# An encoder layer on eight cores: a wider last row block, late queueing of gated products on VectorE, and one more wait on GpSimd

## The chip, the cores and the metric

One Trainium2 chip (trn2), all 8 cores, one launch. The time is the device time of the slowest core in microseconds. A core's span runs from its first to its last instruction in a profiled execution. Some executions fall in a slow state, in which one die runs at a lower clock; only fast runs are compared here, and every profile shown is of a fast run.

## The reference

One layer over x of 4 x 4096 x 1024, float32:

```python
x = x + 0.5 * swiglu(rmsnorm(x, ffn1_norm), ffn1_gate, ffn1_up, ffn1_down)   # hidden 2816
z = rmsnorm(x, mix_norm) @ w_in                                             # q, k, v (512 each), u (1024)
attn_out = chunk_band_attention(q, k, v, rel_bias)                          # 64-row chunks, 576 keys
conv_out = conformer_conv(u, dw_kernel, dw_bias, conv_ln_g, conv_ln_b)      # GLU, conv of 31, LayerNorm, swish
x = x + concatenate([attn_out, conv_out]) @ w_out
x = x + 0.5 * swiglu(rmsnorm(x, ffn2_norm), ffn2_gate, ffn2_up, ffn2_down)
y = rmsnorm(x, final_norm)
```

## The kernel before

Two cores share a sequence. An even core does its first 2176 rows, an odd core the other 1920 and a halo of 512. Rows go through the layer in two groups, and a group in blocks of up to 512 rows, the columns of a matmul:

```python
PLANS = ((((512, False), (384, False), (256, False)),      # even core: group 0
          ((512, False), (256, False), (256, False))),     #            group 1
         (((512, True), (512, False), (256, False)),       # odd core, True is the halo
          ((512, False), (384, False), (256, False))))
```

A Python scheduler holds one stream of work for each part of the layer, estimates the time of each engine, and writes five static instruction queues with semaphore waits. Queues are in order: what stands first in a queue holds up all behind it (the prediction shows a stop of 3.65 us on VectorE that came of it). Where it expects TensorE to wait, it puts filler matmuls.

An FFN piece and a GLU piece each end in an activation on ScalarE and a product on VectorE, which the kernel before queues at once:

```python
ti = nxt("tmpF", 2)
tt = tmpF[:, ti, 0:n]
act(tt, gb, AF.Silu, n, (("ps", bG),), (("tmpF", ti),))
dve(lambda h: h.tensor_tensor(out=at, in0=ub, in1=tt, op=ALU.mult), n,
    (("ps", bU), ("tmpF", ti)), (("AT", gi, fl, s),))
# ... in glu(): channel pieces c, row runs r
todo = [(c, r) for part in (early, late) for c in (0, 1) for r in part]
todo += [(c, r) for c in (2, 3) for r in runs]
# ...
act(tt, bb, AF.Tanh, n, (("ps", bB),), (("rs", ti),), scale=0.5)
dve(lambda h: h.scalar_tensor_tensor(out=gnt, in0=tt, scalar=1.0, in1=ab_,
    op0=ALU.add, op1=ALU.mult), n, (("ps", bA), ("rs", ti)), (("gn", gi_),))
```

After its GLU a group sends the result through DRAM to change its layout, and the convolution reads it back; the scheduler assumes that the return lands 4 us after its bytes. During the first FFN, GpSimd expands the convolution weights, 8 instructions of 4 us, while VectorE writes tables for the attention bias:

```python
P.op("pool", lambda h: h.tensor_tensor(out=o_, in0=i0, in1=i1, op=ALU.mult), 4.1,
     ("cmp", "i32"), (("cwb", i % 2),))                    # waits for i32 only
# ... setup_tables()
dve(lambda h: h.tensor_scalar(out=dst, in0=src, scalar1=rbc, scalar2=None, op0=ALU.subtract), 192,
    ("stage", "cs"), ("cb",))
```

The softmax here doesn't subtract the row's maximum and nothing guards it: scores larger than these inputs give would overflow.

## Time and profile before

| | before |
|---|---|
| time, median of 6 (of all 15 with later rounds; of the 12 fast ones of these) | 1378.92 us (1378.2; 1377.9) |
| spans of the even cores 0, 2, 4, 6 | 1374.7, 1375.3, 1376.2, 1376.4 us |
| spans of the odd cores 1, 3, 5, 7 | 1364.2, 1365.9, 1363.5, 1364.5 us |
| TensorE busy, core 6 | 97% |

The prediction shows most of the lines that matter. Two more kinds are needed later. The first is the view by windows: the stretch, its length, the busy time of TensorE (with instructions), of weight loads, VectorE, ScalarE and GpSimd, then the granted TensorE clock. This is core 6 just after its 3.4 us stop:

```profile
83.80:86.00 2.20, 2.18 (x7) 1.01 (x8) 0.34 (x1) 0.46 (x1) 0.00 (x0) 0.50 1.05 322
```

The clock, third number from the end, is 0.50: after the stop TensorE works at half speed ("half clock" below). The second is an odd core, core 1, where its first convolution begins; the timeline has start, length, instruction, and in brackets the engine's idle time before it and what ended that:

```profile
366.83 5.37 PE L502 MATMUL ps<-dreg,ring 128*128 128x192 bf16 x43 [2.26 <-DMA dreg<-gscr]
```

TensorE waits 2.3 us for the layout's return. In the window 364.0 to 370.4 us of this core the clock was 0.82: the first 16 matmuls came 0.083 us apart, the next 20 came 0.16 us apart, and then they were 0.083 us apart again. So half clock can set in after the stop is over.

### The profile page before, as it was taken

What the parts mean: (1) busy time and instruction counts of PE and PEld (TensorE: products, weight loads), DVE (VectorE), ACT (ScalarE), POOL (GpSimd) and SP (SyncE); (2) the same over time, 40 slices, a digit from 0 to 9 for tenths busy, and PEclk for the clock granted to TensorE, in tenths of its full rate; (3) what the DMA queues carried; (4) which work ended last, traced back from release to release, by engine and by line L of the source; (5) the groups of instructions that cost most, each with busy time, mean ns of one, the idle gap of its engine ahead of it and who ended that gap; (6) DMA issues with size and microseconds to landing.
All of it is one profiled execution on the core that took longest, in us unless ns stands there. A gap on an engine that the chain in (4) does not pass through costs nothing.

```text
span 1376.4 us, 25529 instructions; the slowest of 8 cores (1363.5 to 1376.4 us)
## 1 busy us (share of the span) xinstructions
PE 1337.3 (97%) x9485; PEld 843.3 (61%) x9485; DVE 490.0 (36%) x904; ACT 445.4 (32%) x843; POOL 252.3 (18%) x303
## 2 busy tenths in 40 slices
PE   8999999999999999999999999999999999999995
PEld 4556655565655665656656766766675567666654
DVE  4442222362644432222254522225345253222225
ACT  4311011252477631001245410124438763100123
POOL 2064000340402320000062000006040220000022
PEclk9999999999999999999999999999999999999998
DMA  9386326254740182343311864453674006335413
GB/s 224 72 172 150 62 35 123 43 111 121 160 101 1 33 214 53 71 92 70 70 32 32 213 140 86 75 92 64 151 154 101 18 2 123 64 68 92 81 20 125
DMA packets 33632, 127.72 MB, mean 93 GB/s; under 512 B 3424, under 2 KB 11744, under 8 KB 26464
## 3 DMA queue, kind: packets, MB, share of 16 engines
q0 software_dynamic: 18752, 96.10, 37.0%
q1 hardware_dynamic: 14752, 29.92, 6.8%
q8 instruction: 80, 1.31, 0.4%
q14 instruction: 48, 0.39, 0.1%
HBM read 191.95 MB, written 18.09 MB: 153 GB/s over the span
## 4 chain that ended last, share of the span: by engine, by line
PE 88%; DMA 4%; DVE 3%; issue 2%; ACT 1%; POOL 1%; SPq 0%; DVEq 0%; ACTq 0%; POOLq 0%
PE psA L502 52%; PE ps L502 37%; DMA ring<-wgu 2%; DMA dreg<-gscr 1%; DVE hT L752 1%; DMA gscr<-dreg 1%; DVE xres L752 1%; ACT dreg L512 0%; DVE xres L1415 0%; ACT pb L512 0%; ACT L510 0%; SPq L976 0%; DVE xres L925 0%; DMA xres<-xin 0%; POOL xres L639 0%
## 5 line engine op out<-in xcount | busy, mean ns | idle before, releaser
L502 PE MATMUL psA<-hT,ring 128*128 128x256 bf16 (+2 forms) x4528 | 712.1, 319 | 9.8 <-DVE at L894 3.4
L502 PEld LDWEIGHTS psA<-hT,ring 128*128 128x128 bf16 x4528 | 441.8, 98 | 274.2 <-issue 25.6
L512 ACT ACTIVATE dreg<-psA 128x256 f32<-128x256 f32 (+3 forms) x325 | 170.3, 530 | 670.0 <-PE psA L502 654.4
L502 PE MATMUL ps<-at,ring 128*128 128x256 bf16 (+2 forms) x2112 | 327.1, 317 | 0.0
L894 DVE TENSOR_TENSOR at<-psA,dreg 128x256 bf16<-128x256 f32 (+2 forms) x259 | 138.7, 536 | 476.4 <-PE psA L502 398.2
L502 PEld LDWEIGHTS ps<-at,ring 128*128 128x128 bf16 x2112 | 206.3, 98 | 118.6
L925 DVE SCALAR_TENSOR_TENSOR xres<-ps,xres 128x512 f32<-128x512 f32 (+2 forms) x168 | 89.7, 536 | 168.4 <-PE ps L502 168.3
L695 POOL TENSOR_TENSOR ssum<-ssum,sq 128x256 f32<-128x256 f32 (+2 forms) x108 | 104.7, 970 | 189.3 <-ACT sq L512 186.3
L604 POOL DMA_DIRECT2D ring<-wgu x47 | 28.4, 609 | 513.5 <-PE psA L502 283.6
L502 PE MATMUL ps<-dreg,ring 128*128 128x256 bf16 (+3 forms) x672 | 98.0, 301 | 2.4 <-DMA dreg<-gscr 1.5
L512 ACT ACTIVATE sq<-xres 128x256 bf16<-128x256 f32 (+2 forms) x108 | 55.4, 519 | 96.3 <-DVE xres L925 64.8
L502 PEld LDWEIGHTS ps<-dreg,ring 128*128 128x128 bf16 x672 | 63.5, 98 | 30.9 <-issue 7.2
L752 DVE SCALAR_TENSOR_TENSOR hT<-xres,cs_sb,rstd 128x256 bf16<-128x256 f32 (+2 forms) x120 | 71.2, 642 | 4.7 <-ACT rstd L512 4.7
L502 PE MATMUL ps<-hT,ring 128*128 128x256 bf16 (+2 forms) x368 | 57.5, 312 | 0.0
L512 ACT ACTIVATE dreg<-dreg 128x288 bf16<-128x288 f32 (+8 forms) x84 | 40.4, 480 | 51.3 <-DVE dreg L1021 26.5
L510 ACT ACT_TABLE_LOAD x38 | 48.8, 1283 | 0.7
L502 PEld LDWEIGHTS ps<-hT,ring 128*128 128x128 bf16 x368 | 35.5, 98 | 18.8 <-issue 0.6
L1415 DVE TENSOR_TENSOR xres<-ps,xres 128x256 f32<-128x256 f32 (+2 forms) x48 | 25.1, 531 | 50.1 <-PE ps L502 49.9
L512 ACT ACTIVATE pb<-psA 128x1024 bf16<-128x1024 f32 (+2 forms) x42 | 37.1, 909 | 4.7 <-PE psA L502 4.4
L1434 POOL TENSOR_TENSOR dreg<-pb 128x2304 bf16<-128x2304 bf16 x8 | 32.2, 4050 | 7.1 <-DMA cwscr<-dreg 7.1
L502 PE MATMUL ps<-at,hT 128*128 128x512 bf16 x136 | 31.0, 379 | 0.0
L604 POOL DMA_DIRECT2D ring<-wdA x16 | 8.7, 544 | 119.8 <-PE psA L502 119.8
(85 smaller groups left out, 659.9 us busy)
## 6 DMA issues: line engine op xcount, KB each, us to landing
ring<-wgu POOLq DMA_DIRECT2D x41, 1024.0 KB, 8.9
ring<-wdA POOLq DMA_DIRECT2D x16, 768.0 KB, 9.2
ring<-wdB POOLq DMA_DIRECT2D x16, 640.0 KB, 7.7
ring<-cwscr POOLq DMA_DIRECT2D x16, 576.0 KB, 5.0
cwscr<-dreg SPq DMA_DIRECT2D x8, 576.0 KB, 7.6
ring<-wab POOLq DMA_DIRECT2D x8, 512.0 KB, 7.2
ring<-wout POOLq DMA_DIRECT2D x4, 1024.0 KB, 10.3
yout<-xres SPq DMA_DIRECT2D x2, 2048.0 KB, 11.0
```

The costliest lines, as they stand in the source:

```text
L502: P.op("pe", lambda h: h.matmul(o, lhsT=lhsT, rhs=rhs, start=start, stop=stop, skip_group_check=True), (max(n / 2400.0 + 0.0025, 0.03) if ...
L510: P.op("act", lambda h: h.activation(out=cs[0:1, CS_N + i:CS_N + i + 1], in_=onesS[0:1, 0:1], func=func), 1.5, ("cb1",), ())
L512: P.op("act", lambda h: h.activation(out=out, in_=in_, func=func, **kw), 0.12 + n / 1200.0 + (0.09 * sum(isinstance(v, bass.AP) for v in k ...
L604: P.dma("pool", lambda h, dst=dst, src=src: h.dma_start(out=dst, in_=src), wtok(p, i), (256 if p.reads else 512) * w, reads=p.reads, after ...
L695: pool(lambda h: h.tensor_tensor(out=ss, in0=ss, in1=sqt, op=ALU.add), n, (sk, ("sq", i)), (sk,))
L752: dve(lambda h, dst=dst, xin=xin, gcol=gcol: h.scalar_tensor_tensor(out=dst, in0=xin, scalar=gcol, in1=rt, op0=ALU.mult, op1=ALU.mult), n, ...
L894: dve(lambda h, at=at, ub=ub, tt=tt: h.tensor_tensor(out=at, in0=ub, in1=tt, op=ALU.mult), n, (("ps", bU), ("tmpF", ti)), (("AT", gi, fl, ...
L925: dve(lambda h, xo=xo, xi=xi, bk=bk: h.scalar_tensor_tensor(out=xo, in0=bk, scalar=0.5, in1=xi, op0=ALU.mult, op1=ALU.add), n, (("ps", b), ...
L1415: dve(lambda h, xo=xo, bk=bk: h.tensor_tensor(out=xo, in0=bk, in1=xo, op=ALU.add), n, (("ps", b), xk), (xk,))
L1434: P.op("pool", lambda h, o_=o_, i0=i0: h.tensor_tensor(out=o_, in0=i0, in1=i1, op=ALU.mult), 4.1, ("cmp", "i32"), (("cwb", i % 2),))
```

## The change

Its intent: fewer, wider matmuls in group 1 of the even cores, and fewer stops of TensorE where stages change. The core of the diff (the plumbing that lets a 512-row block be addressed as two of 256 in value/query, attention, output projection and last down stage is cut, and so are other parts at "..."):

```diff
-          ((512, False), (256, False), (256, False))),
+          ((512, False), (512, False, (256, 256)))),
-PREFETCH = (((0, 1, 2),), ((1, 2),))
+PREFETCH = (((0, 1),), ((1, 2),))
 ...
+            def later(ready, taken, emit):
+                pend.update(taken)
+                def gate():
+                    yield ready
+                    emit()
+                    pend.difference_update(taken)
+                S.add(0, gate())
 ...
-                            ti = nxt("tmpF", 2)
+                            ti = nxt("tmpF", 3)
+                            def gated(...):
+                                dve(lambda h: h.tensor_tensor(out=at, in0=ub, in1=tt, op=ALU.mult), ...)
+                            later(lambda ti=ti: P.est("dve", (("tmpF", ti),)) - 0.3, (bG, bU, ("tmpF", ti)), gated)
 ...
-                todo = [(c, r) for part in (early, late) for c in (0, 1) for r in part]
-                todo += [(c, r) for c in (2, 3) for r in runs]
+                todo = [(c, r) for c in (0, 1) for r in early] + [(2, early[0])]
+                todo += [(c, r) for c in (0, 1) for r in late]
+                todo += [(c, r) for c in (2, 3) for r in runs if (c, r) not in todo]
 ...
+                        later(lambda ti=ti: P.est("dve", (("rs", ti),)) - 0.3, (bA, bB, ("rs", ti)), gated)
 ...
-                          issue=0.6, total=4, late=4.0)
+                          issue=0.6, total=4, late=6.0)
 ...
-                         ("cmp", "i32"), (("cwb", i % 2),))
+                         ("cmp", "i32", "cb"), (("cwb", i % 2),))
```

A product is now put into VectorE's queue only when, by the scheduler's clock, its activation is 0.3 us from done. Until then its PSUM banks and buffer count as taken. The scaled copy after a GLU product is always on ScalarE.

## The prediction

> **What bounds the kernel now.** I read first the spans of the cores, because the time is that of the slowest one and the two halves of a sequence run different programs. Even cores do 2176 rows and no halo, odd cores 1920 rows and a 512-row halo for part of the layer.
>
> ```profile
> core 5: 1363.5 us, clock 0.994
> core 6: 1376.4 us, clock 0.991
> core 7: 1364.5 us, clock 0.996
> ...
> die 0 (median of its cores): 1370.3 us, clock 0.994
> die 1 (median of its cores): 1370.4 us, clock 0.993
> ```
>
> All four even cores lie at 1374.7 to 1376.4 and all odd ones at 1363.5 to 1365.9, with both dies at one clock. So the even program sets the time and the odd one follows 10 to 12 us behind. The block plan that the change alters is that of the even program alone: what it gains counts only down to where the odd cores are.
>
> Next, the first part of the page and the chain that ended last, of core 6:
>
> ```profile
> PE 1337.3 (97%) x9485; PEld 843.3 (61%) x9485; DVE 490.0 (36%) x904; ACT 445.4 (32%) x843; POOL 252.3 (18%) x303
> ...
> PE 88%; DMA 4%; DVE 3%; issue 2%; ACT 1%; POOL 1%; SPq 0%; DVEq 0%; ACTq 0%; POOLq 0%
> ```
>
> TensorE is the path for almost the whole span; every other engine has slack. A gain must come from fewer TensorE cycles, or from the few waits that remain. The chain in order of time gives the price of a matmul, in two gate/up stages and two down stages of group 0 (blocks 512, 384, 256) and group 1 (512, 256, 256):
>
> ```profile
> 125.50 46.80 PE ps L502 x288
> ...
> 609.66 78.00 PE psA L502 x480
> ...
> 811.83 41.68 PE ps L502 x288
> 853.51 69.47 PE psA L502 x480
> ```
>
> 480 matmuls over 160 x 1152 columns take 78.00 us, 480 over 160 x 1024 columns 69.47. The difference, 8.53 us for 20480 columns, is 0.4165 ns a column; what is left of 78.00 is 1.23 us, or 2.6 ns a matmul. The down stages agree (5.12 us for 12288 columns). So a 256-wide matmul is not short enough to be bound by its weight load: two of them cost 2.6 ns more than one of 512. The mean durations of the rows by form, 273 ns for 256 columns against 380 for 512, would suggest far more, but they are latencies of pipelined work and must not be subtracted.
>
> Last, who TensorE waited for. On core 6:
>
> ```profile
> PE ps L490 <- DVE cb_sb L1460: 4.9, 1, 4.9
> PE ps L502 <- POOL ssb L700: 3.8, 3, 2.2
> PE psA L502 <- DVE at L894: 3.4, 1, 3.4
> PE psA L502 <- DVE hT L752: 2.9, 5, 0.9
> ```
>
> The first is the start, which stays. The third is one event, and the timeline around 75 us shows it:
>
> ```profile
> 74.57 8.62 DVE L1449 TENSOR_SCALAR cb_sb<-dreg,cs_sb 128x192 bf16<-128x192 f32 x2
> 75.02 8.05 POOL L1434 TENSOR_TENSOR dreg<-pb 128x2304 bf16<-128x2304 bf16 x2
> 83.82 2.40 PE L502 MATMUL psA<-hT,ring 128*128 128x384 bf16 x7 [3.41 <-DVE at L894]
> ```
>
> A table-building pair that takes 0.54 us everywhere else takes 8.62 us while GpSimd runs its two expansions; the gate product queued behind it comes late, and TensorE stands for 3.4 us. The 3.4 us wait on this product is on all four even cores, and core 7 has none: its last such pair is done at 85.6 and its first expansion starts at 88.8.
>
> The fourth is at the entry of the GLU of the convolution:
>
> ```profile
> 969.58 0.42 DVE L1021 SCALAR_TENSOR_TENSOR dreg<-dreg,psA 128x256 bf16<-128x256 f32 x1 [3.65 <-ACT dreg L512]
> 973.92 8.32 PE L502 MATMUL psA<-hT,ring 128*128 128x256 bf16 x46 [0.91 <-DVE hT L752]
> ```
>
> VectorE stands 3.65 us at a GLU product that waits for a tanh, which is itself behind activation table loads; the normalisations of the last block are queued behind it, and TensorE then waits for them.
>
> **What the Trainium skill says.** "SBUF — State Buffer", section "Who interferes with whom": VectorE's second port pair is GpSimd's only one, an exclusive lock held for a whole instruction, and a tensor_scalar in a two-port mode can be blocked by it. The trace agrees: 0.54 us becomes 8.62 beside two expansions of 8.05 together. "TensorE: Matmul & The Clock Gate", section "Back-to-back issue gap": N/2.4 + 2.5 ns, isolated; the same section's sustained 131 ns at N = 512 is not what this case shows (16 of 512 in 3.45 us, 216 ns each). My 2.6 ns agrees with the first. Same page, section "The HAM clock gate (the "warmup" mystery)": after an idle window of about 3.4 us the array runs at half clock, and back at full after as long busy. The trace agrees: after the 3.4 us stop, the 384-wide matmuls start 0.32 us apart, twice the 0.162 of warm ones. "ScalarE: Activation LUTs", section "What ACT_TABLE_LOAD costs": about 1283 ns a load and a drain; the loads here last 1.28 us each and number 38.
>
> **The change part by part.**
>
> 1. Group 1 of the even program is now two blocks of 512, the second split into 256 and 256 only for value/query, attention, output projection and the last down stage. Matmuls saved: gate/up 11 pieces x 2 x 16 = 352 in each of two FFNs, 704; first down stages 12 x 8 x 2 = 192; second down stage of FFN1 10 x 8 = 80; GLU 64; keys 32. Together 1072 x 2.6 ns = 2.8 us, all on the path. Columns, weight bytes and evictions by column stay. Odd cores: nothing.
>
> 2. The expansion on GpSimd now waits for all the table writes too. On even cores the lock is gone: 3.4 us of wait, and what the cold clock costs after it (at half rate for nearly 3 us, so some 1.5 us lost). The expansions start at about 75.2 instead of 75.0, so the weight requests behind them move by next to nothing. 4.9 us on even cores, nothing on odd ones.
>
> 3. Gate products and GLU products are queued on VectorE only when their activation is about to be ready, with a third buffer for the gate so that TensorE may run on. This takes the head-of-line wait away. On core 6 the stops at the two GLU entries are about 1.4 us (group 0, from 306 us) and 3.7 us (group 1, 964 and 972 us together); on core 7 some 4.5 and 1.4 us.
>
> 4. The GLU does channel piece 2 of the first block before the last block is needed: 16 x 216 ns = 3.5 us more of cover for the last normalisation. Against it stands that in group 1 the last block is now 512 wide. Its chain after the last down matmul is, from the rows, residual 0.69, square 0.63, sum 1.16, ones-matmul 0.4, table load and dummy 1.5, Ln 0.57, Exp 0.63, with hand-overs some 6.3 us, then 8 x 0.6 us of normalisation: 11.2 us. The cover was 10.4 us of GLU (768 columns x two pieces) and 1.7 to 2.6 us of keys; it will be 10.4 (512 columns x three pieces) and 1.7. So group 1 is just covered if ScalarE doesn't go back and forth between tanh and Ln (about 1.5 us a change), and loses 1 to 3 us if it does. I count parts 3 and 4 as 2 us gained on even cores and 3 us on odd ones.
>
> 5. The scheduler expects later landings, the scaled GLU copy is always on ScalarE, and the split block's outputs leave as 1 KB runs: 0 to 0.5 us at the tail, against.
>
> Sum for even cores: 2.8 + 4.9 + 2.0 - 0.4 = 9.3 us, to a span of about 1367. Odd cores: about 3, to 1361. The even program stays the slowest. The median time is 2.5 us above the profiled span; it goes from 1378.9 to about 1369.5.
>
> **Rivals.**
>
> A: wide blocks help much more, because each weight load is used twice as long. For it: PEld is 61% busy, and durations fall from 2 x 273 to 380 ns. Against it: the two-stage arithmetic above leaves 2.6 ns a matmul. Even if it were true, the odd cores would hold the time at about 1363 to 1367, a gain of 1%.
>
> B: the wide last block turns its gains into new waits. At each change of stage there is less small work to put between, and a pending product keeps its banks from the free choice; TensorE would stop for 2 to 4 us at the GLU of group 1, at its second FFN and in the tail. For it: the normalisation chain above has hardly any slack. Against: three pieces of look-ahead in gate/up are 20.7 us of work on the first block. It would leave the time at 1373 to 1379.
>
> C: the lock moves. Without the table writes, other VectorE work with two SBUF inputs meets the expansions. Against: the gate product reads one input from PSUM, and from 95 to 120 us it runs at 0.42 to 0.69 us beside them. It would cost the 4.9 us of part 2: 1374.
>
> **Range and chances.** Parts 1 and 2 are well founded, 7.7 us; parts 3 to 5 range from +6 to -5. From this 1363 to 1376; the odd cores close it below. I predict 1369, range 1362 to 1376. 2% faster is 1351.3, which needs some 15 us from the odd cores too, nearly all of the 17 us of waits that core 7's list has after the start: 2%. 2% slower needs a new stop of 35 us: 2%. Within 2%: 96%.
>
> **What would show it.** Even cores: about 1070 fewer matmuls; gate/up stages of group 1 at 69.1 us for 320; no wait for the gate product near 80 us and no table write above 0.6 us; the wait for hT shorter on both kinds of core; even cores at about 1367, odd at 1361. It is wrong if the odd cores become the slowest, if odd cores move more than 6 us, or if a stop of over 3 us stands at the GLU of group 1.

## The result and the profile after

The changed kernel takes 1362.74 us, median of 7 (1362.12 to 1366.87), against 1378.2 us, median of 15, for the kernel before. The ratio is 0.9894, 95% interval 0.9884 to 0.9904. Ratios here are the mean time of one kernel's fast runs over that of the other's of the same rounds, so not quite the ratio of the medians. The gain is clear of noise but less than 2%. The time lies in the predicted range, close to its lower end; the predicted 9.9 us became 15.5 (15.2 against the median of the 12 fast runs before).

The spans of the cores after, three of the eight:

```profile
core 5: 1356.4 us, clock 0.994
core 6: 1361.8 us, clock 0.995
core 7: 1355.6 us, clock 0.996
```

Even cores are now at 1358.1 to 1362.6 us (14 to 17 us less), odd ones at 1354.4 to 1356.5 (7 to 10 less). The even cores still set the time. The chain that ended last, of core 6, has the same two kinds of stage:

```profile
119.54 46.80 PE ps L545 x288
...
601.78 78.00 PE psA L545 x480
...
802.80 41.44 PE ps L545 x192
844.24 69.07 PE psA L545 x320
```

Group 0 is untouched, 46.80 and 78.00 us as before. A gate/up stage of group 1 has 320 matmuls in place of 480 and takes 69.07 us in place of 69.47; a first down stage 41.44 in place of 41.68. Who TensorE waited for, core 6:

```profile
PE ps L533 <- DVE cb_sb L1526: 5.0, 1, 5.0
PE ps L545 <- POOL ssb L749: 3.2, 3, 2.2
...
PE psA L545 <- DVE hT L801: 1.1, 3, 0.5
PE psA L545 <- DVE at L950: 0.9, 1, 0.9
```

The wait for hT fell from 2.9 to 1.1 us. The 3.4 us wait for the gate product is gone; the 0.9 us in this list is another one, at 473 us. The timeline of core 6 shows the table writes and the expansions apart:

```profile
55.01 0.48 DVE L1515 TENSOR_SCALAR cb_sb<-dreg,cs_sb 128x192 bf16<-128x192 f32 x2
...
56.44 8.06 POOL L1500 TENSOR_TENSOR dreg<-pb 128x2304 bf16<-128x2304 bf16 x2
```

All table writes are done by 55.5 us; before, they were spread from 62 to 83 us between gate products. At the GLU of group 1:

```profile
957.88 5.39 DVE L801 SCALAR_TENSOR_TENSOR hT<-xres,cs_sb,rstd 128x512 bf16<-128x512 f32 x8 [0.93 <-ACT rstd L555]
...
963.18 0.68 DVE L1086 SCALAR_TENSOR_TENSOR dreg<-dreg,psA 128x512 bf16<-128x512 f32 x1
963.41 6.85 PE L545 MATMUL psA<-hT,ring 128*128 128x512 bf16 x31 [0.28 <-DVE hT L801]
```

The eight normalisations of the last block now run in one piece and the GLU product comes behind them; TensorE stands 0.28 us here and 1.1 us in three stops at this GLU on core 6. Before, they were cut in pieces by products that waited for a tanh, with VectorE idle for 3.65 us. And the first convolution of core 1:

```profile
362.89 3.31 PE L545 MATMUL ps<-dreg,ring 128*128 128x192 bf16 x38 [0.40 <-DMA dreg<-gscr]
```

To see where time was gained, I worked out from the traces, for each core, how much earlier (negative) TensorE has done the same number of matmul columns than in the profiled run before. Fillers and the ones-matmuls of the statistics are left out. The table gives the steps between six points of the time before, as medians of the four cores of a kind, in us; the same is done for the experiments told below. The first column holds the start, in which two profiles of one kind differ by some 2 us without a cause in the kernel.

How far the other columns can be trusted, the odd cores show: in f3 core 1 issues the instructions of the kernel before in the same order, and in e1 those of the changed kernel. Yet their rows, which are not in the table, are off by 1.4 us in the column to 600 us and 3.0 in all in f3, by 1.7 and 2.8 in e1. In that column lies their first convolution, after which half clock came in some profiles and not in others. Over all fast runs the changed kernel's spans have a median of 1359.9 us on even cores and 1354.0 on odd ones, against 1375.1 and 1362.7 in 23 fast runs of the kernel before: 15.2 and 8.7 us less.

| run against before | cores | to 200: start, FFN1 of group 0 | to 345: its GLU | to 600: its conv, attention, FFN2 begins | to 930: FFNs to group 1 | to 1120: GLU, conv, attention of group 1 | to the end | all |
|---|---|---|---|---|---|---|---|---|
| changed kernel | even | -5.9 | -0.9 | -1.2 | -1.7 | -5.2 | -0.5 | -15.4 |
| | odd | +1.1 | -2.7 | -4.0 | -0.9 | -2.2 | -0.5 | -9.1 |
| old plan (e1) | even | -4.6 | -1.0 | -1.4 | -0.7 | -3.1 | +0.4 | -10.3 |
| no added wait (e2) | even | -5.8 | -2.1 | -0.4 | -1.5 | -5.2 | -0.9 | -15.9 |
| | odd | +9.2 | -3.8 | -3.7 | -0.1 | -1.8 | -0.9 | -1.0 |
| queued at once (e3) | even | -4.6 | -0.7 | +1.0 | -1.4 | +2.1 | -0.8 | -4.4 |
| | odd | +1.8 | -0.9 | -2.5 | +1.6 | -0.5 | -0.3 | -0.8 |
| old GLU order (e4) | even | -5.1 | -1.1 | -1.2 | -1.7 | +1.6 | -1.5 | -9.0 |
| | odd | +1.6 | -2.9 | -3.4 | -0.8 | -2.0 | -0.5 | -7.8 |
| added wait alone (f2) | even | -5.6 | +1.6 | +0.2 | 0.0 | -0.3 | +0.1 | -4.0 |
| plan alone (f3) | even | +1.9 | -0.2 | -0.7 | -1.8 | +2.2 | -0.9 | +0.5 |
| late queueing alone (f4) | even | -6.8 | -0.7 | -1.4 | -0.7 | -2.8 | -0.1 | -12.5 |
| | odd | +8.1 | -2.9 | -4.2 | -0.3 | -1.6 | +0.4 | -0.5 |

### The profile page after: what moved, and what is told of

It reads as the page before. It is cut to its first block, busy times and chain, and to the rows that moved or that the text cites. A ratio compares the mean times of both kernels' runs of the same rounds, so it can differ in the third digit from the quotient of the medians.

```text
span 1362.6 us, 22713 instructions; the slowest of 8 cores (1354.4 to 1362.6 us)
## 1 busy us (share of the span) xinstructions
PE 1321.0 (97%) x8298; PEld 738.4 (54%) x8405; DVE 470.2 (35%) x814; ACT 432.3 (32%) x765; POOL 249.7 (18%) x293
## 4 chain that ended last, share of the span: by engine, by line
PE 88%; DMA 3%; DVE 3%; issue 2%; ACT 2%; POOL 1%; SPq 0%; DVEq 0%; ACTq 0%; POOLq 0%
PE psA L545 51%; PE ps L545 37%; DMA ring<-wgu 2%; DVE hT L801 1%; ACT dreg L555 1%; DMA dreg<-gscr 1%; DVE xres L984 0%; DMA gscr<-dreg 0%; DVE xres L801 0%; DMA xres<-xin 0%; ACT pb L555 0%; DVE xres L1481 0%; ACT rstd L555 0%; POOL xres L688 0%; ACT L553 0%
## 5 line engine op out<-in xcount | busy, mean ns | idle before, releaser
L545 PE MATMUL psA<-hT,ring 128*128 128x512 bf16 (+2 forms) x3705 | 694.1, 347 | 9.1 <-DMA ring<-wgu 2.8
L545 PEld LDWEIGHTS psA<-hT,ring 128*128 128x128 bf16 x3760 | 367.0, 98 | 331.2 <-issue 14.6
L555 ACT ACTIVATE dreg<-psA 128x512 f32<-128x512 f32 (+4 forms) x277 | 162.3, 592 | 667.4 <-PE psA L545 654.2
L545 PE MATMUL ps<-at,ring 128*128 128x512 bf16 (+2 forms) x1816 | 324.6, 339 | 1.5
L950 DVE TENSOR_TENSOR at<-psA,dreg 128x512 bf16<-128x512 f32 (+2 forms) x215 | 131.0, 610 | 453.9 <-PE psA L545 432.1
L545 PEld LDWEIGHTS ps<-at,ring 128*128 128x128 bf16 x1840 | 179.9, 98 | 144.8 <-issue 0.5
L744 POOL TENSOR_TENSOR ssum<-ssum,sq 128x512 f32<-128x512 f32 (+2 forms) x100 | 103.9, 1040 | 183.5 <-ACT sq L555 180.7
L555 ACT ACTIVATE sq<-xres 128x512 bf16<-128x512 f32 (+2 forms) x105 | 55.8, 536 | 102.9 <-DVE xres L984 66.2
L801 DVE SCALAR_TENSOR_TENSOR hT<-xres,cs_sb,rstd 128x512 bf16<-128x512 f32 (+2 forms) x112 | 70.6, 686 | 18.6 <-ACT rstd L555 18.6
L545 PE MATMUL ps<-hT,ring 128*128 128x512 bf16 (+2 forms) x329 | 61.7, 340 | 0.3
```

The lines of the kernel that those rows point to most:

```text
L545: P.op("pe", lambda h: h.matmul(o, lhsT=lhsT, rhs=rhs, start=start, stop=stop, skip_group_check=True), (max(n / 2400.0 + 0.0025, 0.03) if ...
L555: P.op("act", lambda h: h.activation(out=out, in_=in_, func=func, **kw), 0.12 + n / 1200.0 + (0.09 * sum(isinstance(v, bass.AP) for v in k ...
L744: pool(lambda h: h.tensor_tensor(out=ss, in0=ss, in1=sqt, op=ALU.add), n, (sk, ("sq", i)), (sk,))
L801: dve(lambda h, dst=dst, xin=xin, gcol=gcol: h.scalar_tensor_tensor(out=dst, in0=xin, scalar=gcol, in1=rt, op0=ALU.mult, op1=ALU.mult), n, ...
```

## The experiments

My theory after the result was that late queueing is the main part, the port lock is worth 5 us, and the plan 2.7. Rivals: wide blocks do it, or the cover from the GLU order. Twelve kernels were run, all correct, in four timed runs each. The medians here are those of the fast runs; in brackets is the lowest:

| run | median of fast runs (lowest) us | ratio to before, 95% | even spans, profiled run | odd spans, profiled run |
|---|---|---|---|---|
| e1 old plan | 1366.37 (1365.26), 2 of 4 fast | none | 1364.2 to 1366.0 | 1356.1 to 1359.9 |
| e2 no added wait | 1367.65 (1367.47), 2 of 4 fast | none | 1358.3 to 1361.6 | 1362.3 to 1365.9 |
| e3 queued at once | 1375.22 (1374.18), 3 of 4 | 0.9975, 0.9934 to 1.0015 | 1370.5 to 1373.0 | 1360.4 to 1366.2 |
| e4 old GLU order | 1368.24 (1367.5) | 0.9912, 0.9891 to 0.9933 | 1366.1 to 1367.0 | 1355.0 to 1359.2 |
| f1 4 us | 1364.96 (1363.44), 3 of 4 | 0.9903, 0.9884 to 0.9923 | 1359.1 to 1363.7 | 1353.3 to 1355.9 |
| f2 added wait alone | 1375.38 (1374.45), 3 of 4 | 0.999, 0.997 to 1.001 | 1369.7 to 1373.0 | 1361.2 to 1368.7 |
| f3 plan alone | 1379.33 (1377.3) | 1.0014, 0.9998 to 1.0031 | 1374.1 to 1377.3 | 1360.5 to 1362.5 |
| f4 late queueing alone | 1368.64 (1366.83) | 0.994, 0.9924 to 0.9957 | 1361.8 to 1364.0 | 1362.9 to 1365.7 |
| g1 GLU products late only | 1366.11 (1365.75), 3 of 4 | 0.9919, 0.9896 to 0.9943 | 1360.3 to 1364.0 | 1354.0 to 1361.0 |
| g2 later statistics | 1362.09 (1361.41), 3 of 4 | 0.9892, 0.9868 to 0.9916 | 1356.4 to 1359.1 | 1350.2 to 1353.1 |
| g3 tail order | 1368.67 (1367.92), 3 of 4 | 0.9934, 0.991 to 0.9958 | 1364.9 to 1368.2 | 1360.3 to 1363.0 |
| h1 later statistics, not at projections | 1361.48 (1360.19) | 0.9872, 0.9854 to 0.9889 | 1356.4 to 1359.7 | 1348.0 to 1350.8 |

### e1: the old block plan in the changed kernel

```diff
-          ((512, False), (512, False, (256, 256)))),
+          ((512, False), (256, False), (256, False))),
-PREFETCH = (((0, 1),), ((1, 2),))
+PREFETCH = (((0, 1, 2),), ((1, 2),))
```

> The changed kernel with group 1 of the even program put back to blocks of 512, 256 and 256; everything else of the change stays. Theory (2.6 ns a matmul): even cores lose 2.5 to 3.5 us against the changed kernel, spread evenly over the stages of group 1, odd cores lose nothing; time about 1365 to 1366. Rival (wide blocks are the main gain of the even cores, which gained 16 us where I had 9): even cores lose 6 us or more, time 1369 or above.

Of its timed runs too few were fast for a ratio; the two fast ones took 1365.26 and 1367.48 us. From the table, even cores gain 5.7 us after the first 200 us, against 9.5 in the changed kernel: the plan is worth 3.8 us there. About half of it stands between 930 and 1120 us, the rest in the FFNs. Over the fast runs even spans are 3.9 us longer than the changed kernel's. The theory holds, the rival (6 us or more) falls; the size is a little over my 3.5.

### e2: the changed kernel without the added wait

```diff
-                         ("cmp", "i32", "cb"), (("cwb", i % 2),))
+                         ("cmp", "i32"), (("cwb", i % 2),))
```

> The changed kernel without the added wait of the GpSimd expansions for the table writes. Theory (port lock): a table write of about 8 us and a stop of TensorE of 3 to 4 us come back near 80 us on even cores, plus some 1.5 us at half clock; even cores lose about 5 us, odd ones nothing; time about 1367. Rival (the new order of the VectorE queue puts the table writes ahead of the expansions by itself): no table write above 0.6 us, no core moves by over 1 us, time 1363.

Neither theory had all of this. As the rival said, the even cores lose nothing: the new queue order alone puts their table writes ahead. The odd cores lose 8.1 us by 200 us, +9.2 against +1.1. The timeline of core 1:

```profile
62.86 4.39 DVE L1515 TENSOR_SCALAR cb_sb<-dreg,cs_sb 128x192 bf16<-128x192 f32 x2
63.09 8.05 POOL L1500 TENSOR_TENSOR dreg<-pb 128x2304 bf16<-128x2304 bf16 x2 [44.73 <-DVE pb L1509]
67.25 8.65 DVE L1515 TENSOR_SCALAR cb_sb<-dreg,cs_sb 128x192 bf16<-128x192 f32 x2
...
77.60 17.59 PE L545 MATMUL psA<-hT,ring 128*128 128x512 bf16 x78 [7.14 <-DVE at L950]
```

The new queue order brings the expansions of the odd cores forward, from 88.8 us (core 7 before) to 63.1, into their table writes. These take 4.4 and 8.7 us in place of 0.5, and TensorE stands 7.1 us. So the lock is real, and the added wait is what keeps it off the odd cores, which would otherwise be the slowest.

### e3: products queued at once in the changed kernel

```diff
-                pend.update(taken)
-                def gate(): ...
-                S.add(0, gate())
+                emit()
```

> The changed kernel with gate and GLU products queued on VectorE at once again, as in the kernel before; third buffer, GLU order and the rest stay. Theory (a product waiting for its activation holds up the normalisations behind it): the waits for hT at the GLU entries come back, even and odd cores lose 3 to 6 us; time 1366 to 1369. Rival (the cover of 3.5 us from the GLU order is enough by itself): below 1.5 us on all cores, time 1363 to 1364.

The time is 1375.22 us, with a ratio of 0.9975 nearly that of the kernel before: more is lost than expected. Core 0 of this run, who TensorE waited for:

```profile
PE psA L539 <- DVE hT L795: 4.9, 12, 0.8
...
PE psA L539 <- DMA ring<-wgu: 3.9, 4, 1.7
```

The wait for hT is 4.9 us, against 0.5 on core 0 of the changed kernel. Against the changed kernel's rows of the table, the even cores lose 2.2 us in the column to 600 us and 7.3 in that to 1120, the odd ones 1.8, 1.5, 2.5 and 1.7 in the four middle columns. Part of the 7.3 us is half clock, which three of the four even cores show at 970 to 974 us. The theory holds, and its numbers were too small. As the third buffer stays in this run, that buffer by itself is not what gained.

### e4: the old GLU order in the changed kernel

```diff
-                todo = [(c, r) for c in (0, 1) for r in early] + [(2, early[0])]
-                todo += [(c, r) for c in (0, 1) for r in late]
-                todo += [(c, r) for c in (2, 3) for r in runs if (c, r) not in todo]
+                todo = [(c, r) for part in (early, late) for c in (0, 1) for r in part]
+                todo += [(c, r) for c in (2, 3) for r in runs]
```

> The changed kernel with the old order of the GLU pieces; late queueing stays. Theory (queue order does most): even cores lose 1 to 3 us, odd ones 1 to 3 us; time 1364 to 1366. Rival (the cover does most): even cores lose 4 us or more at the GLU of group 1, whose last block is now 512 wide, odd cores 4 us or more at the GLU of group 0; time 1367 or above.

The rival is right for the even cores, and neither is right for the odd ones. Even cores lose 5.5 to 5.8 us at one place, 964 us, where TensorE takes each matmul at the pace of the normalisations (core 0):

```profile
958.89 5.38 DVE L801 SCALAR_TENSOR_TENSOR hT<-xres,cs_sb,rstd 128x512 bf16<-128x512 f32 x8
959.89 0.38 PE L545 MATMUL psA<-hT,ring 128*128 128x512 bf16 x1 [0.62 <-DVE hT L801]
...
961.10 0.38 PE L545 MATMUL psA<-hT,ring 128*128 128x512 bf16 x1 [0.29 <-DVE hT L801]
```

Some 1.7 us of the loss is half clock, which followed these stops. The same core by windows:

```profile
964.00:967.50 3.50, 3.21 (x9) 1.16 (x9) 0.27 (x1) 0.60 (x1) 0.00 (x0) 0.51 0.28 50
```

Odd cores show no loss after the start. The piece moved ahead is the first run of the group, and in group 0 of the odd cores that is the 32 history columns of the convolution, 16 short matmuls; their group 1, whose last block is 256 wide, shows no loss either, nor does the even cores' group 0. The order belongs to the plan: it pays for the wide last block of group 1.

### f1: the assumed landing back at 4 us

```diff
-                          issue=0.6, total=4, late=6.0)
+                          issue=0.6, total=4, late=4.0)
```

> The changed kernel with the scheduler's assumed landing time of the GLU's second transfer back from 6 to 4 us. Theory (with 4 us the convolution is put into TensorE's order before its input has landed; TensorE stops for over 2 us and then runs at half clock): odd cores lose 3 to 5 us at the first convolution, near 365 us, even cores under 1 us; as the even cores are the slowest, the time stays within 1.5 us of 1363. Rival (the gain there came from the queue order): no core loses over 1 us there.

Missed, the theory and for the even cores the rival too. Stops at the first convolution are given as the time between the starts of two matmuls, less what the first takes warm; the idle time in the profile's lines is some 0.2 us less. On odd cores the stop at the first convolution stays at 0.0 to 0.3 us; on even ones it goes from 0.7 to 1.2 us up to 2.4 to 2.7. The time is 1364.96 us, ratio 0.9903 against 0.9894, with intervals that overlap. So, as far as the traces show, 6 us serves the even cores, whose GLU would otherwise end too near its convolution; what removed the stop on odd cores is the queue order, as f4 shows again (0.0 on all four with 4 us).

### f2: the added wait alone, in the kernel before

```diff
-                         ("cmp", "i32"), (("cwb", i % 2),))
+                         ("cmp", "i32", "cb"), (("cwb", i % 2),))
```

> The kernel before with nothing but the added wait of the GpSimd expansions for the table writes. Theory (port lock, with the old queue order on even cores): even cores gain about 5 us near 80 us, odd cores nothing; even spans 1369 to 1372, time 1372 to 1374. Rival (the lock is put off, or the later expansions hold up weight requests): even cores gain less than 2 us.

The step between 75 and 92 us is -5.25 us on cores 0 and 2 and -6.5 on cores 4 and 6: the lock and the half clock after it are gone, as the theory says. But the time is 1375.38 us, ratio 0.999, and neither forecast holds: over the fast runs even spans are 2.3 us shorter than those of the kernel before in the same rounds, and odd ones, where I expected nothing and core 1 issues its instructions in the same order, 3.6 us longer. The latter is not explained. On core 0 this stands among the waits:

```profile
PE ps L502 <- DMA dreg<-gscr: 2.5, 2, 2.0
```

The stop at the first convolution rose from 0.4 to 0.7 us before to 2.0 to 2.2 on the four even cores, and core 0 ran at half clock after it: 1.5 to 3.2 us were given back at the next stage set by transfers. On core 0 the last store of the layout change took 5.42 us, before 4.84, and the return 7.60, before 6.65. Why these transfers were longer in this run is not settled; with 6 us in place of 4 the changed kernel has the shorter stop at this place (f1).

### f3: the plan alone

Old order, products at once, 4 us, old choice of engine, no added wait; the split of the block and the third buffer stay.

```diff
-                pend.update(taken) ... S.add(0, gate())
+                emit()
-                todo = [(c, r) for c in (0, 1) for r in early] + [(2, early[0])] ...
+                todo = [(c, r) for part in (early, late) for c in (0, 1) for r in part] ...
-late=6.0   ("cmp", "i32", "cb")   if True:
+late=4.0   ("cmp", "i32")         if P.t["act"] < P.t["dve"]:
```

> The changed kernel with everything but the block plan put back (queueing at once, old GLU order, 4 us, old choice of engine, no added wait; the third gate buffer stays). Theory (the wide last block needs the other parts): even cores gain 2.7 us of matmuls and lose 4 to 8 us at the GLU of group 1, where the last normalisation is then not covered; even cores at 1378 to 1382, time 1380 to 1384, slower than before; odd cores as before within 1 us. Rival (the plan carries its own gain): even cores 2 to 3 us faster than before.

Ratio 1.0014: the plan alone gains nothing. In the table the even cores gain 1.8 us in the column to 930 us and lose 2.2 in that to 1120; around the GLU (930 to 1000 us) the loss is 3.5 us, just under what I expected. What the plan's matmuls gain is lost again at the GLU of group 1.

### f4: late queueing alone

The kernel before with late queueing and the third buffer, the rest old:

```diff
-          ((512, False), (512, False, (256, 256)))),
+          ((512, False), (256, False), (256, False))),
 ...
-                todo = [(c, r) for c in (0, 1) for r in early] + [(2, early[0])] ...
+                todo = [(c, r) for part in (early, late) for c in (0, 1) for r in part] ...
-late=6.0   ("cmp", "i32", "cb")   if True:
+late=4.0   ("cmp", "i32")         if P.t["act"] < P.t["dve"]:
```

> The kernel before plus the late queueing of the products and the third buffer alone (old plan, old GLU order, 4 us, no added wait). Theory: even cores gain 5 us near 80 us, since the new queue order puts the table writes ahead of the expansions there, and 4 to 6 us at the GLU entries, to 1364 to 1367; on odd cores the lock comes in, plus 9 us near 75 us against 3 us gained at the GLU entries, to 1369 to 1372, so the odd cores are the slowest, time 1371 to 1374. Rival (late queueing helps both kinds alike): odd cores at 1360 to 1362, time about 1367.

Even cores at 1361.8 to 1364.0 us: this part alone makes 12.5 of their 15.4 us, the 5 us of the lock among them. Odd cores meet the lock; core 1:

```profile
PE psA L545 <- DVE at L950: 7.9, 2, 7.1
```

They lose 8.1 us to 200 us, and gain 8.6 after it where I expected 3. So odd cores end at 1362.9 to 1365.7, not at 1369 to 1372, and the time is 1368.64, between what theory and rival forecast. Of the 8.6 us up to 3 can be scatter (see above the table of steps): over the fast runs odd spans are 1.8 us longer than those of the kernel before in the same rounds, not 0.5 shorter.

### g1: late queueing for the GLU only

```diff
-                            later(lambda ti=ti: P.est("dve", (("tmpF", ti),)) - 0.3, (bG, bU, ("tmpF", ti)), gated)
+                            gated()
```

> The changed kernel with only the gate products of the two FFNs queued at once again; the GLU products stay late. Theory (the hold-up is at the GLU entries, where activation table loads delay the tanh): no core loses over 2 us, time 1363 to 1365. Rival (late gate products matter too, as FFN pieces run beside the normalisations where blocks change): even cores lose 3 us or more in the first FFN and where an FFN begins, odd cores 3 us or more; time 1366 or above.

1366.11 us, ratio 0.9919 against 0.9894: about 3.4 us worse than the changed kernel, at the rival's edge, with intervals that overlap slightly. On all four even cores TensorE waits 0.7 us for normalised rows at 45 to 49 us, in the first FFN, where blocks still arrive; the changed kernel has no such wait there. The GLU's products matter more (e3 loses 11 us on even cores, this run 2.5); that the gate's matter too is likely, not certain.

### g2, g3 and h1: looking for a better version

g2 places the ones-matmul of every normalisation later in TensorE's queue:

```diff
-                    yield lambda: max(P.est("pe", tuple(k for k, o in lst)) + 0.5, fb_est()) if free_rstd else INF
+                    yield lambda: max(P.est("pe", tuple(k for k, o in lst)) + 1.5, fb_est()) if free_rstd else INF
```

> The changed kernel with one number altered: the ones-matmul of a normalisation is placed in TensorE's order 1.5 us after the scheduler's estimate of its sum on GpSimd, not 0.5 us. Theory (the sums take 1.47 us where the scheduler assumes 0.95, so TensorE stops 1.1 us at such a matmul near 276 us on even cores and three times on odd ones): even cores gain about 1.3 us, odd ones 2 to 3; time 1361 to 1362. Rival (the later statistics push the normalisations into the GLU entries): even cores lose 1 to 3 us at the GLU of group 1, time 1364 to 1366.

1362.09 us, ratio 0.9892. In the profile, odd cores gain 3.8 us and even ones 2.5 against the changed kernel, but even cores lose 2.2 of it back between 930 and 1000 us and odd ones 2.7 at the GLU of group 0. Theory and rival both show, at different places.

g3 queues the final normalisations of group 1 singly and only on an empty VectorE queue:

```diff
+                    if idx == 3 and gi == 1:
+                        yield lambda: max(P.est("dve", (("rstd", rr),)) - 0.3, P.t["dve"] + 0.3)
-                    if kc % 2 == 0:
+                    elif kc % 2 == 0:
```

> The changed kernel in which the final normalisations of group 1 are queued on VectorE singly and only when its queue is empty, so that the residual sums of the last block go first. Theory (at the end TensorE waits 2.2 us for a sum because the last residuals stand behind normalisations): the end comes 1 to 2 us earlier on even cores, time 1361 to 1362. Rival (VectorE is full there, so the order only moves the work): within 0.5 us of the changed kernel, or up to 2 us later, time 1363 to 1365.

A clear miss, 1368.67 us. Core 0 of this run:

```profile
1342.61 0.42 DVE L986 SCALAR_TENSOR_TENSOR xres<-ps,xres 128x256 f32<-128x256 f32 x1 [0.67 <-ACT ssb L555]
1342.95 11.71 DVE L803 SCALAR_TENSOR_TENSOR xres<-xres,cs_sb,rstd 128x512 f32<-128x512 f32 x24
```

The residuals do go first, and VectorE sat idle 0.67 us between them; then all 24 normalisations stand at the end in one block of 11.7 us. The place "behind the residuals" was behind all of them.

h1 is g2 without the normalisations ahead of the projections:

```diff
-                    yield lambda: max(P.est("pe", tuple(k for k, o in lst)) + 0.5, fb_est()) if free_rstd else INF
+                    yield lambda: max(P.est("pe", tuple(k for k, o in lst)) + (0.5 if idx == 1 else 1.5), fb_est()) if free_rstd else INF
```

> The changed kernel with the later place of the ones-matmul (1.5 us after the estimated sum) for all normalisations but those ahead of the projections, which keep 0.5. Theory (in the run with 1.5 us everywhere the losses of 2 to 3 us stood at the GLU entries, which the kept 0.5 avoids, the gains elsewhere): even cores gain 2 to 4 us against the changed kernel, odd ones 4 to 7; even spans 1355 to 1359, time 1359 to 1361, ratio to before near 0.987. Rival (what moved was noise of start and transfers): time 1362 to 1364, ratio 0.989.

1361.48 us, ratio 0.9872: the fastest kernel run here, 1.3 us of median under the changed kernel and 0.6 under g2; its interval (0.9854 to 0.9889) and that of the changed kernel (0.9884 to 0.9904) just touch, and they were not timed in the same rounds. Even cores gain 2.7 us and odd ones 6.1 in the profile, as the theory had it.

Not tried: late queueing with two buffers, and the scaled copy always on ScalarE by itself.

## Why the prediction was right or wrong

**What bounds the kernel, and part 1.** Right. The even cores set the time before and after. The price of 2.6 ns a matmul gave 69.1 us for a gate/up stage of 320, and the chain shows 69.07. The even cores issue 1080 matmuls less. e1 and f3 bear out that wide blocks are not the main gain, so rival A falls.

**Part 2.** Its size was nearly right and its account half wrong. On even cores the step at that place is -5.25 us on cores 0 and 2 and -6.5 on cores 4 and 6, against 4.9. The 4.9 was read from core 6, and there it was a misreading: after the stop 19 matmuls in a row took 6.0 us at half clock (83.8 to 89.8 us) where 3.1 is warm, which costs 2.9 us, not 1.5. On cores 0 and 2 it cost 1.7 us. With a stop of 3.6 us between the starts, the two sums are 6.5 and 5.25. Also, late queueing removes the lock there too (e2, f4), so the added wait is not what the even cores owe it to. And "nothing on odd ones" was wrong in the changed kernel: without the wait the odd cores lose 8 us (e2), because the lock moves. Rival C had the moving lock; it looked for it in VectorE work with two inputs from SBUF, and it came in the table writes of the other program.

**Parts 3 and 4 are the step that failed, by their size.** "I count parts 3 and 4 as 2 us gained on even cores and 3 us on odd ones." After the first 200 us the even cores gained 9.5 us; if 2.8 of it are part 1, 6.7 are left for parts 3 to 5. The odd cores gained 10.3. Three things were missing from the term. First, I found stops of 5.1 us on core 6 and 5.9 on core 7 at the GLU entries and booked less than half of them on even cores and half on odd ones; e3 and f4 show that late queueing gives most of them back. Second, I left out the stop at the first convolution, though it stood in the list of waits: 2.2 to 2.6 us on odd cores, and after three of those four stops half clock for 1.6 us more. It went with the queue order, by 4.0 us in that column, a part of it the chance of the half clock (in f3, with the same instruction order as before, no odd core had it there and the column shows -1.4 us). Third, half clock follows a run of short stops too: at the GLU of group 1 core 0 before lost 2.5 us in six stops and 1.6 us more at half clock; core 2 shows it too. In the changed kernel's profile no core runs at half clock between 45 and 1340 us, where seven of eight did before.

**The cover of part 4** was credited to every core. e4 shows it in one place only, group 1 of the even cores, where it is worth 5.5 to 5.8 us and is needed for the wide block. The chain of 11.2 us against 12.1 of cover was nearly exact: it just fits, and TensorE stood 0.5 to 1.5 us there.

**Rival B** (the wide block's gain turns into a wait) is what f3 shows, and the other parts are what prevents it (e3, e4).

By its own list the prediction was wrong in one point: odd cores moved by more than 6 us (9.1 in the profile, 8.7 over the fast runs). That the time still fell into the range owes something to the width of the range: the term for parts 3 and 4 was less than a third of what came, on both kinds of core. "Within 2%" was right: the odd cores stood only 12 us below the even ones, and 2% is 27.6 us.

## What to carry to other kernels

In a static in-order queue, an instruction that waits for another engine should be queued when its input is nearly there, not when it is known: here that was worth most of the gain, on an engine that is 36% busy. When such a change moves work on one engine, look at what shares a port with it in every program of the launch; a wait that looks idle may guard the program that is not the slowest yet. Count a stop of TensorE with the half clock that may follow it, and expect a wide last block to need its own cover at the next stage.

## What the Trainium skill lacked or had wrong

- "TensorE: Matmul & The Clock Gate", section "The HAM clock gate (the "warmup" mystery)", gives an idle window of about 3.4 us. Of 15 stops of 2.0 to 2.7 us at the first convolution, in the profiles of the kernel before, f1 and f2, 6 were followed by half clock, for 1.5 to 1.6 us more. Stops that short are not safe.
- Same page, "Back-to-back issue gap": the sustained 131 ns a matmul at N = 512 is not seen. A stage of 320 such matmuls, each with its weight load, took 69.07 us, 216 ns each.
- "SBUF — State Buffer" has the lock for the length of one instruction. On the even cores before, one tensor_scalar of 192 columns took 8.40 us, as long as two expansions of 4 us in a row: it did not get in between them. In e2 a pair took 4.39 us and the next 8.65, and three single writes of these took 4.16, 4.02 and 4.71 us, so there each blocked write got in after one expansion.
- "ScalarE: Activation LUTs" counts a drain of about 1380 ns with each table load. Here a load lasts 1.28 us and the next activation starts 0.02 us after it (951.78 and 953.08 us, core 6 after).
